# Order of the SwiGLU operands, banks of the last short products, and order of o's split behind two mixers

## The chip, the cores and the metric

The kernel runs on one core of a Trainium2 chip. The metric is the time of one execution on the device in microseconds (us); the median of several executions is compared. The core has a matmul engine (TensorE, PE in the profile, with its weight loads as PEld), a vector engine (VectorE, DVE), an engine for activations and copies (ScalarE, ACT), GpSimd (POOL), and SyncE (SP), on whose queue nearly all DMAs are issued. Each engine works its own instructions in the order in which they are queued.

## The reference

Two groups of tokens (512 and 256, together T = 768) go through a trunk of two layers with shared weights and model width 1024, all in 32-bit floats:

```python
def even_layer(x, ...):                       # layer 0
    x = x + 0.5 * swiglu(rmsnorm(x, f1_n), f1_g, f1_u, f1_d)
    x = x + mixer_ab(rmsnorm(x, mix_n), w_in, ..., w_out)
    x = x + 0.5 * swiglu(rmsnorm(x, f2_n), f2_g, f2_u, f2_d)
def odd_layer(x, ...):                        # layer 1
    x = x + 0.5 * swiglu(rmsnorm(x, f1_n), f1_g, f1_u, f1_d)
    x = x + mixer_c(rmsnorm(x, mix_n), w_qkv, rpb, w_out)
    x = x + 0.5 * swiglu(rmsnorm(x, f2_n), f2_g, f2_u, f2_d)
def swiglu(h, wg, wu, wd):
    return (silu(h @ wg) * (h @ wu)) @ wd     # hidden width 2816
```

A last RMS norm follows. `mixer_ab` is a spatial gating unit beside windowed attention, with one input and one output projection; `mixer_c` is neighbourhood attention on a grid. Each mixer ends with `o @ w_out` (1024 x 1024) and the addition to x.

## The kernel before

Activations lie transposed: x is eight tiles `x[m]` of 128 features by 768 tokens. The tokens fall into two halves of 384 (`HALVES`, h = 0 and 1). Every float operand of a matmul is split into a high part (a cast on ScalarE, L111, L193 or L340) and a low part (a subtraction on VectorE, L112, L194 or L341), and a product is three matmuls: high by high, low by high, high by low (`mm3`, L173). Weights come by DMA into four buffers (`raw`, L89) and are split into five buffers of high and low halves (`wsplit`, L101).

**SwiGLU** (`ffn`, L391) multiplies by a scheme of Strassen's kind with seven products of half size per pair of hidden tiles. Its operands are made from x: `b11` and `b21` from the first half of the tokens, and `t2`, `t3`, `t1`, `n4` and `b22` that need the second half. `feed` (L312) makes `b11` or `b21` for h = 0; for h = 1 it makes a tile `tmp` (a subtraction on VectorE, L327, for m below 4, a scaling on ScalarE, L329, for the others), and where both tiles of a k are there, it combines them (VectorE, L348) and splits the result into `t2`. `rest` (L350) makes `t3`, `t1`, `n4` and `b22` step by step. All `tmp` tiles, the copies named next and others share one set of `NE` = 30 buffers (`etile`, L309).

The opening of a SwiGLU is `ORDER`: for pairs 0 and 1 the product p1 (with `b11`, for gate and up, two products each), then p2 (with `b21`) for pairs 0 and 1, then the first hidden values of pair 0 (`hidden`, L475), p1 of pair 2, and so on. p1 leaves its result in a PSUM bank ("X"); ScalarE copies it to an `etile` for later use (L497), since p2 then adds onto the same bank. These copies are kept in a list, `self.copied`. After the opening pair 0 goes on with p6 (`t2`), p7 (`t3`), p5 (`t1`), p3 (`b22`), p4 (`n4`).

**What sets the order.** TensorE's instructions run in the order in which the program text issues them. Side work (norms, `rest`, attention) consists of generators that are resumed between matmuls, when a running estimate of TensorE's time (`self.t`) says so: each yields the time until its next step (`spawn`, `tick`). The instructions of the other engines are ordered at compile time by a planner, which takes what is ready, by priority, and priority falls in the order of issue; a block `high_priority` raises it (the copies of L497 and the weight halves for `b11` and `b21` have it). `issue_after(ins)` puts what is issued inside it behind `ins`, on the engine of `ins`.

**The end of a mixer** (`mixer_out`, L792). The mixer's result is `ot`, eight tiles o of 768 tokens. `ready(k)` (L802) splits o_k into `oh` and `ol`, first its first half and then its second, takes a new tile `x[k]` in the place of o_k and, behind the first mixer, issues the DMA that reloads x (L807). The first six k are made ready, and six tiles m of the output are computed from them for both halves (`put`, L809, adds x). When attention has ended, the last two k are made ready. Tiles m = 6 and 7 are computed whole. Then come the **short products**: for each half and each of the first six m, the share of the last two k (six matmuls), which VectorE adds to x (L861), and `final` (L696), which feeds the SwiGLU and sums squares (L216, L217). All take their bank from the pool `mm` (four banks); the other pool, `aux`, also has four. `half_done(h)` (L714) starts the norm of that half and, for h = 1, runs the eight feeds at once and spawns `rest`. In the mixers' case the second half's feeds can't run inside `final`, because the pool that they write is opened later; they are noted in `self.unfed`. The first SwiGLU of the program has a path of its own (`second`, L371), which waits until two copies are issued and puts its feeds and sums of squares behind the second.

Of the kernel before, what the change touches and what calls it, by code (L numbers as in the profile page):

```python
# [9 lines left out]
F32 = mybir.dt.float32  # L10
# [6 lines left out]
P = 128  # L17
# [5 lines left out]
T = TA + TB  # L23
# [26 lines left out]
class Trunk:  # L50
# [294 lines left out]
    def combine(self, out, x, sign, m, other):  # L345

        g, op = (self.gain(m), ALU.subtract) if sign > 0 else (self.gain(m, self.ngains), ALU.add)
        self.nc.vector.scalar_tensor_tensor(out=out, in0=x, scalar=g, in1=other, op0=ALU.mult, op1=op)  # L348

    def rest(self):  # L350

        (a0, a1), (c0, c1) = HALVES
        yield STEPS[0]
        for n in ("t3", "t1", "n4", "b22"):
            for k in range(4):
                if n == "t1":
                    self.gain_split(n, k, self.tmp[k], k)
                elif n == "t3":
                    t = self.etile("tmp")
                    self.combine(t, self.x[k][:, c0:c1], -1, k, self.tmp[k + 4])  # L360
                    self.split(*self.b[n][k], t)
                elif n == "n4":
                    t = self.tmp["t2", k]
                    self.combine(t, self.x[k + 4][:, a0:a1], 1, k + 4, t)
                    self.split(*self.b[n][k], t)
                else:
                    self.split(*self.b[n][k], self.tmp[k + 4])
                yield STEPS[1]
            self.made += [n]
# [344 lines left out]
    def half_done(self, h):  # L714

        if self.nxt[0] == "last":
            self.spawn(self.finish(h))
        else:
            self.spawn(self.norm_rt(h))
            if h:  # L720
                for m in self.unfed:
                    self.feed(m, h)
                self.spawn(self.rest())

    def finish(self, h):
# [66 lines left out]
    def mixer_out(self, name, ot, chain, cols=False):  # L792

        nc = self.nc
        oh, ol = ([self.gp.tile([P, T], F32R, tag=f"x{n}{k}", name=f"o{n}{k}") for k in range(KD)] for n in "hl")
        src = (oh, ol)
        self.x = [None] * KD
        old = {}  # L800

        def ready(k):  # L802
            for c0, c1 in HALVES:
                self.split(oh[k][:, c0:c1], ol[k][:, c0:c1], ot[k][:, c0:c1])
            self.x[k] = self.xp.tile([P, T], F32, tag=f"x{k}", name=f"x{k}")
            if not cols:
                nc.sync.dma_start(self.x[k], self.xd[k])  # L807

        def put(m, h, ps):  # L809

            c0, c1 = HALVES[h]
            x = self.x[m]
            parts = [(c0, c1, x[:, c0:c1], 0)]
            if cols:
                if m not in old:
                    t = self.rawp.tile([P, T], F32, tag="raw", name="xold")
                    nc.sync.dma_start(t, self.xd[m])
                    old.clear()
                    old[m] = [t[:, a:b].rearrange("p (r c) -> p c r", c=64) for a, b in GROUPS]
                a, b = old[m]  # L820
                parts = [(H, TA, a[:, 48:64, :], 8), (TA, T, b, 4)] if h else [(0, H, a[:, 0:48, :], 8)]
            for a, b, xv, rows in parts:
                out, pv = x[:, a:b], ps[:, a - c0 : b - c0]
                if rows:
                    out, pv = (t.rearrange("p (c r) -> p c r", r=rows) for t in (out, pv))
                nc.vector.tensor_tensor(out=out, in0=pv, in1=xv, op=ALU.add)

        early = range(KD - 2)
        for k in early:
            ready(k)  # L830
        for m in early:
            if m % 2 == 0:
                w4 = self.raw(name, 0, 4, m * P, 2 * P)
                w2 = self.unit(name, 4, 2, m * P, 2 * P)
            c = m % 2 * P
            hi, lo = self.wsplit(w4[:, :, c : c + P])
            w = [(hi[:, k, :], lo[:, k, :]) for k in range(4)] + [tuple(t[:, c : c + P] for t in k) for k in w2]
            for h in (0, 1):
                put(m, h, self.proj(w, src, HALVES[h], ks=early))
        self.drain(chain)  # L840
        late = (KD - 2, KD - 1)
        for k in late:
            ready(k)
        self.ffn_open(self.close("mp"))
        self.ffn_tiles()
        self.norm_begin(self.following)
        for m in late:
            wl = self.unit(name, 0, KD, m * P, P)
            for h in (0, 1) if m < KD - 1 else (0,):
                put(m, h, self.proj(wl, src, HALVES[h]))  # L850
                self.final(m, *HALVES[h])
        w = []
        for m, n in ((0, 4), (4, 2)):
            raw = self.raw(name, KD - 2, 2, m * P, n * P)
            w += [self.wsplit(raw[:, :, c : c + 2 * P]) for c in range(0, n * P, 2 * P)]
        for h, (c0, c1) in enumerate(HALVES):
            for m in early:
                st = [tuple(t[:, k, m % 2 * P : m % 2 * P + P] for t in w[m // 2]) for k in (0, 1)]
                ps = self.proj([None] * 6 + st, src, (c0, c1), ks=late)
                x = self.x[m][:, c0:c1]  # L860
                nc.vector.tensor_tensor(out=x, in0=ps[:, :H], in1=x, op=ALU.add)  # L861
                self.final(m, c0, c1)
            if h:
                put(KD - 1, h, self.proj(wl, src, (c0, c1)))
                self.final(KD - 1, c0, c1)
                self.close("xg")
                self.fw = self.open("work", self.other(self.guards["comb"][1]))
            self.half_done(h)
# [691 lines left out]
```

## Time and profile before

| | us |
|---|---|
| median of 3 runs | 2659.05 |
| lowest and highest run | 2657.87 and 2660.11 |
| the profiled execution | 2661.16 |
| its span, first to last instruction | 2659.4 |
| TensorE busy in the span | 2582.3 |
| VectorE busy | 2262.8 |
| ScalarE busy | 1371.3 |

The profile is that of one execution. Times are from the start of the span. A row of a timeline gives start, duration, engine, line, operation, the tile written and the tiles read, and in brackets how long the engine sat idle before it and what ended that. Duration overlaps with the next instruction, so the pitch from start to start is shorter: matmuls of 384 columns that last 0.34 us follow each other every 0.17. Names of tiles are those of the program without their running numbers: `b110h` is the high part of `b11`, k = 0. The granted clock is the share of full speed at which TensorE was let run; over the whole span it was 0.987. The first mixer ends near 785 us, the second near 2141 us; the first SwiGLU opens the span.

### The profile page before, as it was taken

What the parts mean: (1) busy time and instruction counts of PE and PEld (TensorE: products, weight loads), DVE (VectorE), ACT (ScalarE), POOL (GpSimd) and SP (SyncE); (2) the same over time, 40 slices, a digit from 0 to 9 for tenths busy, and PEclk for the clock granted to TensorE, in tenths of its full rate; (3) what the DMA queues carried; (4) which work ended last, traced back from release to release, by engine and by line L of the source; (5) the groups of instructions that cost most, each with busy time, mean ns of one, the idle gap of its engine ahead of it and who ended that gap; (6) DMA issues with size and microseconds to landing.
All of it is one profiled execution on the core that took longest, in us unless ns stands there. A gap on an engine that the chain in (4) does not pass through costs nothing.

```text
span 2659.4 us, 41163 instructions
## 1 busy us (share of the span) xinstructions
PE 2582.3 (97%) x15150; PEld 2513.1 (94%) x15150; DVE 2262.8 (85%) x4748; ACT 1371.3 (52%) x2847; POOL 82.7 (3%) x124
## 2 busy tenths in 40 slices
PE   7999999999999999999999999999999989999997
PEld 6999999977889999999999999988998989999997
DVE  8989889779869988898998888886667699888886
ACT  6545444555746544445654544454555465454443
POOL 0000000000100000000000000002112100000000
PEclk9999999999999999999999999999999999999999
DMA  5333222421222222222222222232221322222221
GB/s 163 118 81 106 71 72 64 156 74 37 84 80 80 80 78 65 80 72 88 80 80 80 64 80 64 82 123 64 62 62 44 100 88 80 80 71 73 67 86 55
DMA packets 82746, 214.80 MB, mean 81 GB/s; under 512 B 19952, under 2 KB 32752, under 8 KB 82544
## 3 DMA queue, kind: packets, MB, share of 16 engines
q1 hardware_dynamic: 82400, 212.14, 26.0%
q8 instruction: 119, 1.95, 0.3%
q14 instruction: 83, 0.68, 0.1%
q10 hardware_dynamic: 144, 0.03, 0.0%
HBM read 202.70 MB, written 15.07 MB: 82 GB/s over the span
## 4 chain that ended last, share of the span: by engine, by line
PE 91%; DVE 5%; ACT 3%; DMA 0%; issue 0%; SPq 0%; DVEq 0%; ACTq 0%
PE ps_mm L137 59%; PE ps_aux L137 32%; PE ps_aux L141 1%; DVE wlo L112 1%; DVE xl L710 1%; ACT whi L111 0%; DMA raw<-in_w 0%; ACT xh L709 0%; DVE x L677 0%; DVE ol L194 0%; ACT sq L216 0%; DVE x L632 0%; ACT p L883 0%; ACT diag L247 0%; DVE tmp L348 0%
## 5 line engine op out<-in xcount | busy, mean ns | idle before, releaser
L111 ACT CAST whi<-s 128x512 fp32r<-128x512 f32 x496 | 302.0, 620 | 378.5 <-DVE s L580 141.2
L111 ACT CAST whi<-raw 128x512 fp32r<-128x512 f32 x512 | 311.7, 618 | 272.4 <-PE ps_mm L137 135.9
L112 DVE TENSOR_TENSOR wlo<-s,whi 128x512 fp32r<-128x512 f32 x496 | 335.1, 685 | 73.2 <-ACT whi L111 72.9
L112 DVE TENSOR_TENSOR wlo<-raw,whi 128x512 fp32r<-128x512 f32 x494 | 336.7, 687 | 33.9 <-ACT whi L111 30.9
L137 PE MATMUL ps_aux<-dt,whi 128*128 128x384 f32 x864 | 221.5, 338 | 0.0
L137 PE MATMUL ps_mm<-db,whi 128*128 128x384 f32 x864 | 221.5, 338 | 0.0
L137 PEld LDWEIGHTS ps_mm<-db,whi 128*128 128x128 f32 x864 | 156.8, 188 | 0.0
L137 PEld LDWEIGHTS ps_aux<-dt,whi 128*128 128x128 f32 x864 | 156.8, 188 | 0.0
L137 PE MATMUL ps_mm<-xh,whi 128*128 128x512 f32 (+1 forms) x416 | 146.8, 353 | 3.0 <-ACT xh L709 3.0
L137 PE MATMUL ps_mm<-db,wlo 128*128 128x384 f32 x432 | 146.0, 338 | 0.0
L137 PE MATMUL ps_aux<-dt,wlo 128*128 128x384 f32 x432 | 146.0, 338 | 0.0
L137 PE MATMUL ps_mm<-xl,whi 128*128 128x512 f32 (+1 forms) x416 | 142.7, 343 | 1.1 <-DVE xl L710 1.1
L137 PE MATMUL ps_mm<-xh,wlo 128*128 128x512 f32 (+1 forms) x416 | 142.3, 342 | 0.0
L467 ACT COPY u<-ps_mm 128x384 f32<-128x384 f32 x176 | 83.6, 475 | 34.5 <-PE ps_mm L137 34.2
L472 DVE TENSOR_TENSOR u<-ps_aux,u 128x384 f32<-128x384 f32 x176 | 96.9, 551 | 5.0 <-PE ps_aux L137 3.9
L580 DVE TENSOR_TENSOR s<-raw,raw 128x512 f32<-128x512 f32 x124 | 83.3, 685 | 20.9 <-DMA raw<-in_w 20.9
L580 DVE TENSOR_TENSOR s<-raw 128x512 f32<-128x512 f32 x124 | 84.8, 685 | 17.2 <-DMA raw<-in_w 16.9
L137 PE MATMUL ps_aux<-dh,whi 128*128 128x384 f32 x384 | 98.5, 338 | 0.7 <-DVE x L677 0.7
L883 ACT ACTIVATE p<-p,st 128x256 f32<-128x256 f32 (+3 forms) x144 | 69.1, 481 | 53.3 <-DVE st L878 53.2
L632 DVE TENSOR_TENSOR x<-ps_aux,x 128x384 f32<-128x384 f32 x160 | 86.3, 552 | 10.9 <-PE ps_aux L137 10.8
L137 PE MATMUL ps_mm<-oh,whi 128*128 128x384 f32 x256 | 90.2, 352 | 5.1 <-DVE x L861 4.0
L137 PEld LDWEIGHTS ps_mm<-xh,whi 128*128 128x128 f32 x416 | 79.4, 191 | 14.2 <-ACT xh L709 4.1
(427 smaller groups left out, 8098.2 us busy)
## 6 DMA issues: line engine op xcount, KB each, us to landing
raw<-in_w SPq DMA_DIRECT2D x342, 512.0 KB, 3.7
xdm<-x SPq DMA_DIRECT2D x16, 384.0 KB, 2.3
x<-in_x SPq DMA_DIRECT2D x16, 192.0 KB, 5.7
x<-xdm SPq DMA_DIRECT2D x8, 384.0 KB, 3.6
xold<-xdm SPq DMA_DIRECT2D x8, 384.0 KB, 3.1
out_y<-y SPq DMA_DIRECT2D x8, 384.0 KB, 2.5
tab<-skew SPq DMA_DIRECT2D x8, 256.0 KB, 4.6
raw<-in_w SPq DMA_DIRECT2D x8, 256.0 KB, 2.6
```

Source lines behind the costliest of these rows:

```text
L111: nc.scalar.copy(hi, src)
L112: (eng or nc.gpsimd).tensor_tensor(out=lo, in0=src, in1=hi.bitcast(F32), op=ALU.subtract)
L137: self.nc.tensor.matmul(out, lhsT=lhsT, rhs=rhs, start=start, stop=stop, **kw)
L141: self.nc.tensor.transpose(out, src, self.ident)
L467: nc.scalar.copy(e[n, out], bank[key, n])
L472: nc.vector.tensor_tensor(out=t, in0=bank[key, n], in1=t, op=ALU.add)
L580: f = lambda o, x, y, op: self.nc.vector.tensor_tensor(out=o, in0=x, in1=y, op=op)
L632: nc.vector.tensor_tensor(out=o, in0=ps, in1=o, op=ALU.add)
L710: nc.vector.scalar_tensor_tensor(out=lo, in0=src, scalar=gain, in1=hi.bitcast(F32), op0=ALU.mult, op1=ALU.subtract)
L883: nc.scalar.activation(outs[i - n0], outs[i - n0], AF.Exp, scale=-1.0, bias=mn[:, i : i + 1], accum_out=sm[:, i : i + 1])
```

## The change

Three edits, all behind or at the end of the mixers:

1. `half_done` no longer runs the noted feeds at once. It spawns `late_feeds`, which waits until two more copies of L497 have been issued, issues the eight feeds behind the second of them (on ScalarE by an explicit order, on the other engines by the order of issue), and then goes on with `rest`. Where nothing was noted, `rest` is spawned as before.
2. `ready` takes a list of k. It splits the first half of every o in the list, then the second halves, and only then takes the x tiles and issues the reloads.
3. The short products of odd m take their bank from `aux`, those of even m from `mm`.

```diff
+    def late_feeds(self, n):
+
+        while len(self.copied) < n:
+            yield 0.2
+        with self.tc.issue_after(self.copied[n - 1]):
+            for m in self.unfed:
+                self.feed(m, 1)
+        yield from self.rest()
+
     def rest(self):
...
             self.spawn(self.norm_rt(h))
-            if h:
-                for m in self.unfed:
-                    self.feed(m, h)
+            if h and self.unfed:
+                self.spawn(self.late_feeds(len(self.copied) + 2))
+            elif h:
                 self.spawn(self.rest())
...
-        def ready(k):
+        def ready(ks):
             for c0, c1 in HALVES:
-                self.split(oh[k][:, c0:c1], ol[k][:, c0:c1], ot[k][:, c0:c1])
-            self.x[k] = self.xp.tile([P, T], F32, tag=f"x{k}", name=f"x{k}")
-            if not cols:
-                nc.sync.dma_start(self.x[k], self.xd[k])
+                for k in ks:
+                    self.split(oh[k][:, c0:c1], ol[k][:, c0:c1], ot[k][:, c0:c1])
+            for k in ks:
+                self.x[k] = self.xp.tile([P, T], F32, tag=f"x{k}", name=f"x{k}")
+                if not cols:
+                    nc.sync.dma_start(self.x[k], self.xd[k])
...
         early = range(KD - 2)
-        for k in early:
-            ready(k)
+        ready(early)
...
         late = (KD - 2, KD - 1)
-        for k in late:
-            ready(k)
+        ready(late)
...
-                ps = self.proj([None] * 6 + st, src, (c0, c1), ks=late)
+                ps = self.proj([None] * 6 + st, src, (c0, c1), self.psum(self.aux, "aux") if m % 2 else None, late)
```

## The prediction

> **What bounds the kernel now.** I read the page first, then TensorE's waits around the ends of the two mixers, then the windows there, and last the timelines of single engines. On the page TensorE is the bound, and the chain that ended last is nearly all matmuls:
>
> ```profile
> PE 2582.3 (97%) x15150; PEld 2513.1 (94%) x15150; DVE 2262.8 (85%) x4748; ACT 1371.3 (52%) x2847; POOL 82.7 (3%) x124
> ...
> PE 91%; DVE 5%; ACT 3%; DMA 0%; issue 0%; SPq 0%; DVEq 0%; ACTq 0%
> ```
>
> The matmuls stay the same, so only TensorE's 77 us without work (2659.4 - 2582.3) and its time at a slow clock can be won. What TensorE waits for behind the first mixer (690 to 860 us; columns: total us, times, longest):
>
> ```profile
> PE ps_mm L137 <- ACT p L497: 4.2, 1, 4.2
> PE ps_mm L137 <- DVE x L861: 2.0, 2, 1.8
> PE ps_mm L137 <- DVE ol L194: 1.1, 3, 0.6
> PE ps_mm L137 <- ACT oh L193: 1.1, 1, 1.1
> ```
>
> Behind the second (2040 to 2200 us):
>
> ```profile
> PE ps_mm L137 <- ACT p L497: 4.7, 1, 4.7
> PE ps_mm L137 <- DVE x L861: 2.0, 2, 1.8
> ...
> PE ps_mm L137 <- DVE ol L194: 0.5, 1, 0.5
> ```
>
> The three edits aim at these: the copies of the first products (L497), the adds that free the banks of the short products (L861), the split of o (L193, L194). The windows of both places (stretch, length, then PE, PEld, DVE, ACT and POOL busy, granted clock, DMA) show what a wait costs beside itself, and what VectorE does meanwhile:
>
> ```profile
> 764.00:785.30 21.30, 19.29 (x103) 18.65 (x102) 18.50 (x41) 11.98 (x24) 0.00 (x0) 0.92 0.04 17
> 785.30:808.30 23.00, 18.85 (x100) 18.53 (x99) 22.77 (x56) 19.74 (x41) 0.00 (x0) 0.93 0.31 102
> 808.30:824.30 16.00, 15.98 (x93) 15.37 (x92) 13.90 (x30) 8.83 (x19) 0.00 (x0) 1.00 0.17 52
> 2120.00:2140.90 20.90, 18.89 (x101) 18.25 (x100) 18.42 (x41) 12.38 (x25) 0.00 (x0) 0.92 0.07 28
> 2140.90:2166.20 25.30, 20.60 (x102) 20.23 (x101) 24.33 (x58) 20.02 (x41) 0.00 (x0) 0.87 0.38 125
> 2166.20:2182.00 15.80, 15.80 (x95) 15.80 (x95) 15.42 (x35) 9.33 (x19) 0.00 (x0) 1.00 0.21 63
> ```
>
> TensorE pauses 2.01 (21.30 - 19.29) and 4.15 us behind the first mixer, 2.01 and 4.70 behind the second, and around each pause its clock is down: 19.29 x 0.08 = 1.5, 18.85 x 0.07 = 1.3, 18.89 x 0.08 = 1.5, 20.60 x 0.13 = 2.7 us lost. That is 9.0 and 10.9 us of TensorE's time. But VectorE is idle for only 2.80 + 0.23 + 2.10 = 5.13 us in the first three stretches and 2.48 + 0.97 + 0.38 = 3.83 in the others. It is the engine that comes next.
>
> **The change, part by part.** No instruction is added or removed; the order and the banks change.
>
> *The feeds.* The four first products run from 785.33 to about 793.65, so one takes 2.08 us; the first copy starts only at 797.44. ScalarE, 19.74 of 23.00 us busy there, has it in line behind feeds. Behind the first mixer, and in the opening SwiGLU, such a late copy comes just after VectorE's fourth combine of the feeds (L348):
>
> ```profile
> 785.33 0.34 PE L137 MATMUL ps_mm<-b110h,whi 128*128 128x384 f32 x1
> 793.48 0.34 PE L137 MATMUL ps_mm<-b113h,wlo 128*128 128x384 f32 x1
> 797.33 0.60 DVE L348 SCALAR_TENSOR_TENSOR tmp<-tmp,ngains 128x384 f32<-128x384 f32 x1
> 797.44 0.48 ACT L497 COPY p<-ps_mm 128x384 f32<-128x384 f32 x1
> ...
> 15.28 0.48 ACT L497 COPY p<-ps_mm 128x384 f32<-128x384 f32 x1
> 29.70 0.61 DVE L348 SCALAR_TENSOR_TENSOR tmp<-tmp,ngains 128x384 f32<-128x384 f32 x1
> 29.82 0.46 ACT L497 COPY p<-ps_mm 128x384 f32<-128x384 f32 x1
> 30.34 0.69 PE L137 MATMUL ps_mm<-b210h,whi 128*128 128x384 f32 x1 [6.01 <-ACT p L497]
> ```
>
> Copies and feeds write the same set of 30 buffers, and I infer that a copy does not get its buffer before the feeds issued ahead of it. The change issues two copies first and the twelve feed buffers after them, as the opening does: there the second copy is prompt (15.28), and the third waits for the feeds. So the first copy's 4.15 and 4.70 us go, and the **third copy** is late next. Queued on ScalarE behind the second copy are four scalings and four casts of the feeds, then the sixteen of `rest`; TensorE asks for these only after twelve products. The third copy is due after six products, 12.5 us from the first one's start, 13.1 with the norm's two matmuls. The second copy ends at 4.2 + 0.5; then the feeds need VectorE for 4 x 0.47 + 4 x 0.53 us (the pitch of instructions that take 0.55 and 0.61), 1.4 for three low parts in between and 1.8 to 2.4 for weight halves: 7.2 to 7.8, so the third copy starts at 11.9 to 12.5. I take no wait for it; the other bound is the opening's, 29.82 - 15.28 = 14.5 us behind the second copy, so at 18.7 and over 5 us of wait.
>
> *The banks.* Twelve short products of 1.04 us (six matmuls) meet four banks, while in the first half VectorE needs about 1.5 us for each (an add, a low part, a sum of 0.47 to 0.53 us pitch):
>
> ```profile
> 765.11 0.56 DVE L861 TENSOR_TENSOR x<-ps_mm,x 128x384 f32<-128x384 f32 x1 [0.48 <-PE ps_mm L137]
> 776.72 0.45 PE L137 MATMUL ps_mm<-oh,whi 128*128 128x384 f32 x1 [1.80 <-DVE x L861]
> 778.31 0.52 PE L137 MATMUL ps_mm<-ol,whi 128*128 128x384 f32 x1
> ...
> 2120.61 0.56 DVE L861 TENSOR_TENSOR x<-ps_mm,x 128x384 f32<-128x384 f32 x1 [0.20 <-PE ps_mm L137]
> ```
>
> With eight banks TensorE runs ahead: 2.01 + 1.5 = 3.5 us sooner at the first product, behind either mixer. The second pool was the attention's, which has ended by then, so using it costs nothing; were it not free, a bank wait of up to 1.8 us would stay.
>
> After this pause of 1.80 us the matmuls take 0.52 us, not 0.34. The Trainium skill (TensorE: Matmul & The Clock Gate, Part 1: The HAM clock gate) puts the fall to half rate behind an idle window of about 3.4 us. By that rule this pause costs only itself, and taking it away would win 2.0 us per mixer in place of 3.5; the row has slow matmuls after 1.80 us, so the measurement decides.
>
> *The split of o.* TensorE's first product wants the first halves of six o's; now each o's second half stands in between. Removed: up to 1.1 + 1.1 us at the first mixer and 0.5 at the second; nothing, if the second halves are then late instead. I take 1.8 + 0.2, near the upper end, because the first six slots of both engines then hold what the first product wants. The reloads of x are issued behind all splits, and the next weights stand behind them in SP's queue:
>
> ```profile
> 699.95 9.76 SPq L807 DMA_DIRECT2D x<-xdm  x6
> ```
>
> The sixth reload waits for the same last split as now, so the queue clears at the same time. The first goes some 4 us later; four free banks hide that, and without them the first add would be late by about as much.
>
> *Where the gain of the first two stops.* VectorE's feed work can start only behind the second copy, and TensorE takes weight halves hot from VectorE:
>
> ```profile
> 787.23 0.55 DVE L327 TENSOR_TENSOR tmp<-x 128x384 f32<-128x384 f32 x1
> 813.46 0.69 DVE L580 TENSOR_TENSOR s<-raw 128x512 f32<-128x512 f32 x1 [2.10 <-DMA raw<-in_w]
> 823.59 0.68 DVE L112 TENSOR_TENSOR wlo<-s,whi 128x512 fp32r<-128x512 f32 x1
> 824.32 0.44 PE L137 MATMUL ps_mm<-t30h,wlo 128*128 128x384 f32 x1
> ...
> 2179.15 0.68 DVE L112 TENSOR_TENSOR wlo<-s,whi 128x512 fp32r<-128x512 f32 x1
> 2181.27 0.34 PE L137 MATMUL ps_mm<-t30h,wlo 128*128 128x384 f32 x1
> ```
>
> The half written until 824.27 is used at 824.32: no slack, with nearly all feed work ahead of it on VectorE, and, by the order of issue, still ahead of it after the change. So at this point TensorE can win only what VectorE loses of idle time, not 9.0 us. Of the 5.13 I leave 0.48 ahead of the first add and half of the 2.10 for a weight DMA, whose buffer comes free with TensorE's progress: 3.6. Of the second's 3.83 I leave 0.20 and half of 0.97 + 0.38: 2.95; there the same half is ready 1.4 us before its use, of which I add half: 3.7. Both could be 0, or the full 9.0 and 10.9.
>
> Sum: 2.0 + 3.6 + 3.7 = 9.3 us. The profiled execution took 2661.16 us (its span of 2659.4 and 1.8 around it), so 2651.9 of its kind. It lies 2.1 above the median of the runs shown, 2659.05; from the median, **2649.8**.
>
> **Rivals.** *All waits vanish.* If the work of `rest` falls behind the urgent halves, VectorE is no bound: 9.0 + 10.9 + 2.7 (all of the split) = 22.6 us, 2636.5. For it: `rest` is issued more than two products later than now. Against: the hot half at 824.27.
>
> *VectorE is held as well*, so that the change moves the waits and little else. The products start at 785.33 - 3.5 = 781.8, the second copy ends at 786.5, a scaling of 0.5 us leads the feeds: they start on VectorE at 787.0, against 787.23 now. If nothing fills VectorE until then, its idle time only moves, and 2.0 + 0.2 + 0.7 stay: 2656.2. For it: the feed buffers are taken in order, and a scaling on ScalarE has the first. Against: the norm's short chain and two weight halves are ready to fill the hole.
>
> *The opening's course*, the slower side. There the third copy holds TensorE for 6.01 us, and what follows is late as well:
>
> ```profile
> 19.32 0.72 PE L137 MATMUL ps_aux<-ones,acc 128*128 128x1 f32 x6
> 33.22 0.55 DVE L217 TENSOR_TENSOR acc<-acc,sq 128x384 f32<-128x384 f32 x1
> 59.81 0.34 PE L137 MATMUL ps_aux<-t10h,whi 128*128 128x384 f32 x1
> ...
> 826.16 0.34 PE L137 MATMUL ps_aux<-t10h,whi 128*128 128x384 f32 x1
> ...
> 2183.00 0.34 PE L137 MATMUL ps_aux<-t10h,whi 128*128 128x384 f32 x1
> ```
>
> From the end of the four first products to t1's product the opening takes 59.81 - 19.32 = 40.5 us, the mixers 826.16 - 793.65 = 32.5 and 2183.00 - 2149.3 = 33.7. At the opening's pace the change would lose 8.0 + 6.8 = 14.8 us there and win 7.0 (banks) and 2.0 (split): 5.8 slower, 2664.9. It decides from where the third copy starts more than some 10 us behind the second. Against: the opening still sums squares then (L217, until 33.22), which the mixers' ends have done before.
>
> **Chances and range.** Forecast (5.3 to 14 us won) 0.50; all waits vanish 0.17; VectorE held 0.25; the opening's course 0.08. About 0.2%, 5.3 us, is what a measurement of this kernel can tell from no change. Faster 0.67 is the first two, same 0.26 the third and a little of the last, slower 0.07. The range, 2641 to 2658, holds the forecast's own (2645 to 2653.7), the held case, and the lower part of the first rival.
>
> **What would show it.** Right: no wait on L861; first and second copies within 1 us of their products; VectorE over 97% busy from the first product to t3's, and TensorE waiting in that stretch for hidden values, weight halves or the third copy; no wait on oh over 0.5 us. Wrong: no such waits at all (then near 2637), or a wait of 5 us or more for the third copy on either side (then no gain, or slower).

## The result and the profile after

| kernel | median, us | range, us | ratio to before, 95% interval |
|---|---|---|---|
| before | 2658.42 | 2655.55 to 2660.11 | |
| after | 2650.89 | 2649.77 to 2652.01 | 0.9970 (0.9961 to 0.9978) |

The change is 7.5 us faster; the forecast was 2649.8. The two profiled spans differ by 9.2 us (2659.4 to 2650.2). The page of the kernel after, its busy times and its chain:

```profile
PE 2574.1 (97%) x15150; PEld 2503.7 (94%) x15150; DVE 2259.8 (85%) x4748; ACT 1371.4 (52%) x2847; POOL 82.9 (3%) x124
...
PE 89%; DVE 7%; ACT 2%; issue 1%; DMA 1%; SPq 0%; DVEq 0%; ACTq 0%
```

TensorE is busy 8.2 us less for the same matmuls, and its time without work is 76.1 us (2650.2 - 2574.1) where it was 77.1: in this pair of traces most of the gain is clock, and the waits have changed places more than they have gone. The granted clock over the whole span, pauses included, points the same way in every execution: 0.990 to 0.991 in the eight of the kernel after, 0.986 to 0.990 in the 103 of the kernel before that were timed beside the experiments. In the chain VectorE has more (7% in place of 5%). What TensorE waits for behind the first mixer (680 to 860 us):

```profile
PE ps_mm L137 <- ACT p L506: 2.6, 1, 2.6
PE ps_mm L137 <- ACT oh L193: 1.4, 1, 1.4
PE ps_mm L137 <- DVE wlo L112: 1.3, 2, 1.0
PE ps_mm L137 <- DVE sg L490: 0.8, 1, 0.8
```

and behind the second (2030 to 2200 us):

```profile
PE ps_mm L137 <- ACT whi L111: 1.9, 1, 1.9
...
PE ps_mm L137 <- DVE sg L490: 1.4, 1, 1.4
PE ps_mm L137 <- DVE wlo L112: 1.4, 2, 1.0
...
PE ps_mm L137 <- ACT p L506: 0.4, 1, 0.4
```

The waits on banks (the adds, now L870) and for the first copies (now L506) are gone. In their place stand the third copy, hidden values (sg), weight halves (wlo), and behind the second mixer weights (whi). Their places, with the copies in front of them, in the timeline of the kernel after:

```profile
779.43 0.34 PE L137 MATMUL ps_mm<-b110h,whi 128*128 128x384 f32 x1
782.19 0.48 ACT L506 COPY p<-ps_mm 128x384 f32<-128x384 f32 x1
784.15 0.47 ACT L506 COPY p<-ps_mm 128x384 f32<-128x384 f32 x1
786.04 0.55 DVE L217 TENSOR_TENSOR acc<-acc,sq 128x384 f32<-128x384 f32 x1
790.47 0.60 DVE L341 SCALAR_TENSOR_TENSOR t10l<-tmp,gains,t10h 128x384 fp32r<-128x384 f32 x1
794.82 0.61 DVE L348 SCALAR_TENSOR_TENSOR tmp<-tmp,ngains 128x384 f32<-128x384 f32 x1
795.25 0.47 ACT L506 COPY p<-ps_mm 128x384 f32<-128x384 f32 x1
795.77 0.44 PE L137 MATMUL ps_mm<-b210h,whi 128*128 128x384 f32 x1 [2.65 <-ACT p L506]
801.04 0.44 PE L137 MATMUL ps_mm<-b110h,whi 128*128 128x384 f32 x1 [0.83 <-DVE sg L490]
818.97 0.45 PE L137 MATMUL ps_mm<-t30h,wlo 128*128 128x384 f32 x1
...
2130.00 0.34 PE L137 MATMUL ps_mm<-b110h,whi 128*128 128x384 f32 x1
2138.38 0.44 PE L137 MATMUL ps_mm<-b110h,whi 128*128 128x384 f32 x1 [1.86 <-ACT whi L111]
2171.47 0.44 PE L137 MATMUL ps_mm<-t30h,wlo 128*128 128x384 f32 x1
```

Set beside the same matmuls before (785.33, 824.32, 2140.9 and 2181.27 in the prediction), TensorE reaches the first product 5.9 us sooner, and t3's second product, where the hot half is used, 5.35 us sooner; at the second mixer 10.9 and 9.8, of which 6.7 were there when its short products began. Each mixer wins and then gives a part back.

To see what VectorE did in that, take the stretch from the first short products to t3's second product, cut at the same matmuls in both kernels. Before:

```profile
763.17:824.32 61.15, 54.95 (x297) 53.37 (x296) 55.19 (x125) 40.57 (x83) 0.00 (x0) 0.94 0.18 60
2113.83:2181.26 67.43, 60.72 (x325) 59.71 (x325) 58.77 (x133) 42.54 (x87) 2.59 (x2) 0.92 0.26 82
```

After, with the stretch from the first product to t3 (for the second mixer to just behind it) once more by itself, in two parts:

```profile
761.42:818.97 57.55, 52.25 (x297) 50.20 (x296) 54.92 (x129) 41.04 (x84) 0.00 (x0) 1.00 0.22 64
2107.12:2171.47 64.35, 59.11 (x325) 56.73 (x324) 56.49 (x132) 41.94 (x86) 2.58 (x2) 0.97 0.25 82
...
779.40:801.00 21.60, 17.76 (x100) 16.80 (x98) 21.34 (x54) 18.60 (x40) 0.00 (x0) 1.00 0.47 126
801.00:816.50 15.50, 14.16 (x80) 13.38 (x80) 14.95 (x34) 10.11 (x20) 0.00 (x0) 1.00 0.08 30
2129.40:2152.90 23.50, 20.36 (x103) 19.06 (x101) 21.64 (x53) 18.41 (x40) 0.00 (x0) 0.93 0.42 140
2152.90:2170.30 17.40, 15.38 (x87) 14.61 (x88) 16.87 (x40) 11.17 (x22) 0.00 (x0) 1.00 0.06 24
```

The first stretch is 3.60 us shorter (TensorE waits 0.9 us less in it, and 2.7 are clock), and VectorE's idle time in it fell from 5.96 to 2.63 us: nearly all of the gain. The second is 3.08 us shorter, but VectorE's idle time fell only from 8.66 to 7.86. There 2.28 us of VectorE's work are no longer in the stretch. With 1.3 us from the split the two make 8.0 us. The rest of the 9.2 lies outside: 0.4 us ahead of the first mixer's end, 1.4 between the two stretches, and 0.6 lost behind the second; one trace of each kernel can't tell what of that comes from the edits.

Cut once more at the first product, TensorE gains 4.15 us at either mixer from the first short product to there, and loses 0.55 and 1.1 us from there to t3's product, where it waits longer than before (5.3 us in place of 4.2, and 5.2 in place of 4.7). All that the two stretches gain arises ahead of the first products; putting the feeds later keeps more of it than the banks alone keep (below).

### The profile page after: what moved, and what is told of

The parts are those of the page before. It is cut to its first block, busy times and chain, and to the rows that moved or that the text cites. A ratio compares the mean times of both kernels' runs of the same rounds, so it can differ in the third digit from the quotient of the medians.

```text
span 2650.2 us, 41138 instructions
## 1 busy us (share of the span) xinstructions
PE 2574.1 (97%) x15150; PEld 2503.7 (94%) x15150; DVE 2259.8 (85%) x4748; ACT 1371.4 (52%) x2847; POOL 82.9 (3%) x124
## 4 chain that ended last, share of the span: by engine, by line
PE 89%; DVE 7%; ACT 2%; issue 1%; DMA 1%; SPq 0%; DVEq 0%; ACTq 0%
PE ps_mm L137 56%; PE ps_aux L137 32%; DVE wlo L112 1%; PE ps_aux L141 1%; DVE x L641 1%; DVE s L589 1%; DVE xl L719 1%; DMA raw<-in_w 1%; DVE tmp L348 0%; ACT whi L111 0%; ACT xh L718 0%; DVE x L686 0%; ACT sq L216 0%; ACT p L892 0%; DVE sg L493 0%
## 5 line engine op out<-in xcount | busy, mean ns | idle before, releaser
L641 DVE TENSOR_TENSOR x<-ps_mm,x 128x384 f32<-128x384 f32 x160 | 87.1, 551 | 6.0 <-PE ps_mm L137 5.8
```

Source lines behind the costliest of these rows:

```text
L641: nc.vector.tensor_tensor(out=o, in0=ps, in1=o, op=ALU.add)
```

## The experiments

Each was timed beside the kernel before on the same chip (its median there 2659.3 to 2659.5, for the last run 2657.8). Two theories stand against each other in most of them: that VectorE's load sets the end of these stretches (A), and that single waits do, each of which can be taken away (the rivals).

**The split alone.** Only the diff's `ready` is applied.

> The kernel before with only the split of o changed (all first halves, then all second halves, then the reloads of x). Theory A, that the term stands by itself: the shift of TensorE's matmuls between the two profiles was 1.3 us in front of the first mixer's first product (and 0.2 at the second), so 2656.9 to 2657.0 beside 2658.4. The prediction's own term was 2.0, so 2656.4. Rival: the first mixer's gain is eaten by what comes next (a bank's add late by the later reload of x, or the feeds), no difference within 0.5 us; then waits on L861 grow by about what the waits on oh and ol lost.

Measured: 2656.85, ratio 0.9990 (0.9981 to 0.9999). By the same matmuls of both traces the step at the first mixer's products is 1.35 us, at the second 0: there the wait for ol (0.5 us) went, but one for the attention's row values (st, L878) grew from 0.7 to 1.6 us, as it did in the kernel after. The waits on L861 did not grow (2.0 us at either mixer), so the rival's sign is missing. The rest of the measured difference cannot be told from its interval.

**The banks alone.**

```diff
-                ps = self.proj([None] * 6 + st, src, (c0, c1), ks=late)
+                ps = self.proj([None] * 6 + st, src, (c0, c1), self.psum(self.aux, "aux") if m % 2 else None, late)
```

> The kernel before with only the second PSUM pool for every other short product. Theory A (VectorE is the next bound and the first copy stays behind the feeds): TensorE comes 3.5 to 4.2 us sooner to the first product behind each mixer, but the wait for the first copy (4.2 and 4.7 us) grows by what VectorE cannot gain; VectorE has 2.80 and 2.48 us of idle time there, so 1.5 to 2.3 us per mixer stay: 3 to 4.6 us in all, 2653.8 to 2655.4. Rival B (the banks' gain is TensorE's own and stays): 4.2 + 4.2 = 8.4, near 2650. Rival C (the copy's wait grows by all of it): no difference within 1 us, first copy at the same time as before.

Measured: 2657.60, ratio 0.9994 (0.9985 to 1.0002). Its waits, first mixer and then second:

```profile
PE ps_mm L137 <- ACT p L497: 6.7, 1, 6.7
...
PE ps_mm L137 <- ACT p L497: 5.3, 1, 5.3
PE ps_mm L137 <- ACT whi L111: 1.4, 1, 1.4
```

The first copy's wait grew from 4.2 to 6.7 and from 4.7 to 5.3 us, and the wait for weights appears behind the second mixer. About 2 us per mixer are left of the 4.15 by the same matmuls, as theory A has it; B, 8.4 us, falls. The time alone does not tell A from C, but in the trace the first copy behind the first mixer starts 1.6 us sooner, counted from the first short product, where C has it at the same time.

**The feeds alone.** `late_feeds` and its call are applied; banks and split are as before.

> The kernel before with only the feeds put behind the second copy. Theory A (VectorE is the next bound): the first copy's waits (4.15 and 4.70 us) go, but TensorE waits again behind them (third copy, hidden values, weight halves) and keeps only VectorE's idle time there, 0.23 + 1.05 and 1.15, so 1.3 to 2.5 us in all: 2656 to 2657. Rival B (waits and slow clock of these stretches are all won): 4.15 + 1.3 + 4.70 + 2.7 = 12.9, 2645.5. Rival C: without the banks VectorE has to wait for the second copy with nothing to do (its feeds now start behind it), so that the time is as before or up to 2 us longer.

Measured: 2658.27, ratio 0.9997 (0.9988 to 1.0006). B falls. Its waits, first mixer and then second:

```profile
PE ps_mm L137 <- DVE sg L490: 1.7, 1, 1.7
...
PE ps_mm L137 <- ACT p L506: 4.4, 1, 4.4
```

By the same matmuls the first mixer's stretch is 2.8 us shorter. But 1.6 of these lie ahead of the first product, where the edit changes nothing: there a pause on a bank was followed by the slow clock in the trace before and not in this one (last section). That leaves 1.2 us for the feeds. Behind the second mixer the third copy now holds TensorE for 4.4 us, nearly what the first copy did before (4.7), and that stretch became 1.8 us longer (69.23 against 67.43). This is the rival of the opening's course in small. The time does not tell A from C. With the banks, in the kernel after, the third copy's wait there is 0.4.

The three ratios together are 0.0019 below one, the change 0.0030; with 0.0009 of uncertainty on each, it can't be told whether the parts add.

**Own buffers for the copies.** Four buffers that the down projection uses only later take the first four copies, in the kernel before and in the kernel after:

```diff
-                        e[n, "p1"] = etile("p1")
+                        j = 2 * p + names.index(n)
+                        e[n, "p1"] = etile("p1") if j > 3 else self.fw.tile([P, H], F32, tag=f"p1{j}", name=f"p1{j}")
```

> The kernel before, with the feeds where they were, but the copies of the first four first products written to four buffers that the down projection uses only later, not to the 30 shared with the feeds. Theory of the shared buffers: the copies are then prompt (each within 1.5 us of its product's end) though the feeds are issued ahead of them, in the opening too, where the third copy holds TensorE for 6.0 us. Rival: the copies stand behind the feeds for another reason (ScalarE's line); then the first copy behind the mixer still starts just after the fourth combine and the time does not move. If the copies are prompt: with VectorE as the next bound 2 to 6 us less than before (2652 to 2656); if TensorE alone counts 4.15 + 4.70 + 6.0 and the clock, 15 us or more (2643 or less).

Measured: 2657.08, ratio 0.9995 (0.9986 to 1.0004). Its timeline, the opening and then behind the first mixer:

```profile
17.84 0.47 ACT L498 COPY p<-ps_mm 128x384 f32<-128x384 f32 x1
34.29 0.69 PE L137 MATMUL ps_aux<-diag,onesr 128*128 128x384 f32 x1 [5.72 <-DVE diag L249]
...
788.22 0.48 ACT L498 COPY p<-ps_mm 128x384 f32<-128x384 f32 x1
805.20 0.44 PE L137 MATMUL ps_mm<-b110h,whi 128*128 128x384 f32 x1 [1.21 <-DVE sg L481]
```

The copies are prompt although the feeds are still issued ahead of them: 788.22 in place of 797.44 behind the mixer, and in the opening the third one at 17.84 in place of 29.82. So the shared buffers did set the order. In the opening the 6.01 us for the third copy became 5.72 for the norm's matrix: nothing is won there. The 15 us that were to come if TensorE's waits alone count did not, and the interval (at most 3.7 us won) leaves only the lower end of the 2 to 6 us.

> The kernel after, with the copies of the first four first products in four buffers of their own (those of the down projection's sums). If shared buffers put the third copy behind the feeds, it is now within 1.5 us of its product's end and its wait of 2.65 us behind the first mixer (0.4 behind the second) and of 6.0 us in the opening goes. Theory A (VectorE next): the waits for hidden values and weight halves grow by nearly as much, 0.997 again, at most 1 us less. Rival D (the third copy's place is what costs): 2.6 + 0.4 us or more less, 0.9955 to 0.996. In the opening both expect nothing, as the wait for the norm took all of it back.

Measured: 2653.68, ratio 0.9981 (0.9972 to 0.9990). The waits for the third copy are gone, and this one stands in their place behind the first mixer:

```profile
801.20 0.49 PE L137 MATMUL ps_mm<-b110h,whi 128*128 128x384 f32 x1 [3.33 <-DVE sg L490]
```

2.65 + 0.83 us before the third pair's first product became 3.33: D falls.

**Low parts on GpSimd**, which is idle there:

```diff
-                    self.split(*self.b[n][k], t)
+                    self.split(*self.b[n][k], t, eng)
```

(`eng` is `nc.gpsimd` behind the mixers only; n4, and b22 in the same way. `split` gives it the subtraction, not the cast.)

> The kernel after, with the low parts of n4 and b22 behind the two mixers computed on GpSimd in place of VectorE (8 x 0.47 = 3.8 us off VectorE per mixer; about 1.0 us each on GpSimd by the row of the last norm). The kernel after stands at 0.997 of before. Theory A (VectorE is the bound from the first products to t3): TensorE wins 2 to 4 us per mixer more, in the waits for hidden values and weight halves (0.8 + 1.3 us behind the first, 1.4 + 1.4 behind the second, and clock), ratio 0.995 to 0.996. Rival D (ScalarE's line is the bound, since the third copy waits behind 19 scalings and casts with no idle time on ScalarE): the third copy's 2.65 us stay and the time does not move, 0.997. Rival E: GpSimd slows VectorE or is itself late for b22, waits on b22 or n4 over 1 us, 0.998 or more.

Measured: 2658.58, ratio 0.9997 (0.9988 to 1.0006): the change's gain is gone. VectorE and GpSimd in that run, and the first stretch (761.82 to 822.70 by the same matmuls):

```profile
796.57 1.35 POOL L194 TENSOR_TENSOR b220l<-tmp,b220h 128x384 fp32r<-128x384 f32 x1 [8.68 <-ACT b220h L193]
796.97 1.37 DVE L348 SCALAR_TENSOR_TENSOR tmp<-x,ngains,tmp 128x384 f32<-128x384 f32 x1
...
798.26 1.36 DVE L194 TENSOR_TENSOR t23l<-tmp,t23h 128x384 fp32r<-128x384 f32 x1
809.12 0.55 DVE L490 TENSOR_TENSOR sg<-ps_mm,acc 128x384 f32<-128x384 f32 x1
...
761.82:822.70 60.88, 54.06 (x298) 51.89 (x297) 58.80 (x122) 41.63 (x85) 10.57 (x8) 0.97 0.23 68
```

The VectorE instructions of 384 columns with both inputs in SBUF that start while GpSimd works take about 1.36 us in place of 0.55 to 0.61. The one at 809.12, which takes an input from PSUM, started while GpSimd worked (808.10 to 810.09) and took 0.55. VectorE lost more than it was spared: it is busy 58.80 us, 3.9 more than in the kernel after, and the stretch is 3.3 longer. This is rival E, and at the same time a load added to VectorE that TensorE had to wait out.

**Later work.** On ScalarE t1's scalings are put behind the fourth copy, and the casts of n4 and b22 behind the sixth (`first` is the third copy's place in the list):

```diff
+            if first and n != "t3":
+                i = first + (1 if n == "t1" else 3)
+                while len(self.copied) <= i:
+                    yield 0.2
+                behind = lambda i=i: self.tc.issue_after(self.copied[i])
             for k in range(4):
+              with behind():
```

> The kernel after, with the scalings and casts of t1 behind the fourth copy and those of n4 and b22 behind the sixth on ScalarE. No work is saved; 5.9 us of VectorE work per mixer (n4's four combines, eight low parts) and ten casts leave the stretch up to t3. Theory A (VectorE bound in that stretch, but not behind it): TensorE wins 2 to 5 us per mixer, ratio 0.993 to 0.996, waits for the third copy, hidden values and weight halves mostly gone. Rival F (VectorE is as full behind t3): the waits come back at n4, b22 or the weight halves there, 0.997. Rival G: n4 or b22 late, waits over 2 us on them, 0.998 or more.

Measured: 2652.37, ratio 0.9973 (0.9964 to 0.9982), as the kernel after. VectorE and TensorE there:

```profile
794.50 2.49 DVE L112 TENSOR_TENSOR wlo<-raw,whi 128x512 fp32r<-128x512 f32 x4
799.90 0.55 DVE L194 TENSOR_TENSOR t33l<-tmp,t33h 128x384 fp32r<-128x384 f32 x1
800.37 0.55 DVE L497 TENSOR_TENSOR sg<-ps_mm,acc 128x384 f32<-128x384 f32 x1
801.06 0.47 PE L137 MATMUL ps_mm<-b110h,whi 128*128 128x384 f32 x1 [4.01 <-DVE sg L497]
```

Behind the first mixer the third copy and the weight halves hold nothing up now; sg does, 4.0 us, behind t3's work in VectorE's order. The 2 to 5 us per mixer of theory A did not come.

> Both: n4 and b22 late and their low parts on GpSimd. Theory A: as the better of the two, or up to 2 us more, 0.992 to 0.995. Rival F (load behind t3 limits the late order): this one is clearly (over 2 us) below the late order alone. Rival D (ScalarE's line): equal to the late order alone within 1 us.

Measured: 2660.82, ratio 1.0005 (0.9996 to 1.0014). GpSimd costs as much as in the run above, 8.5 us over the late order alone. None of the three theories had that sign.

**t3 behind sg.** VectorE does t3's combines and low parts only after the first pair's sg and v (`self.hid` lists the instructions that write v).

```diff
+        while len(self.hid) <= i:
+            yield 0.2
+        yield from self.rest(self.hid[i])
...
+              with self.tc.issue_after(behind) if behind and n == "t3" else nullcontext():
```

> The kernel after, with t3's combines and low parts put behind the first pair's hidden multiplies (sg and v) in VectorE's order, behind both mixers. No work is saved or taken out of the stretch up to t3. Theory A (VectorE's load up to t3 sets the end): the waits for sg (0.8 and 1.4 us) go and come back at the weight halves or at t3, ratio 0.9965 to 0.9975 as the kernel after. Theory H (it is VectorE's order: sg stands in line behind values that are needed more than 10 us later): 2 to 4 us less than the kernel after, 0.9955 to 0.9963, no wait on sg and none on t3 over 0.5 us.

Measured: 2658.83, ratio 0.9999 (0.9990 to 1.0008). Its waits behind the first mixer up to 900 us, its first stretch, and what follows:

```profile
PE ps_mm L138 <- ACT whi L112: 4.5, 4, 1.5
...
761.11:816.71 55.60, 51.72 (x297) 50.44 (x297) 53.06 (x122) 40.03 (x82) 0.00 (x0) 1.00 0.23 66
816.71:838.03 21.32, 18.54 (x99) 16.64 (x98) 20.52 (x49) 9.89 (x22) 0.00 (x0) 1.00 0.38 109
```

sg's wait went, and TensorE was 2 us quicker up to t3 (55.60 against 57.55). Behind it VectorE is still full (20.52 of 21.32), sums of weights are late, and TensorE waits for their casts: both theories fall, the work only changes its place, at a loss.

> The late order of t1, n4 and b22, and t3 behind sg and v. In the late order alone TensorE waited 4.0 and 3.3 us for sg and the third copy no more, and the weight halves before t3 hardly (0 and 0.4 us). Theory A (load up to t3): with n4 and b22 gone from that stretch VectorE has room, so 7.3 us of waits and about 2 us of slow clock are won: 4 to 8 us less than the kernel after, 0.994 to 0.9955. Theory H says the same. Rival F (VectorE as full behind t3, where n4 and b22 now stand): waits on t1, n4, b22 or weight halves behind t3 come to 5 us or more and the ratio stays at 0.997.

Measured: 2661.43, ratio 1.0002 (0.9993 to 1.0010).

> The same, with the first four copies in buffers of their own. The late order has taken the third copy's wait already, so within 1 us of the run without own buffers behind the mixers; in the opening the 6.0 us wait moves to the norm's matrix (as in the two runs with own buffers, where nothing stayed). If the shared buffers still cost something behind the mixers, 1 us or more less.

Measured: 2660.94, ratio 1.0007 (0.9999 to 1.0016). In both the same waits for whi appear (5.4 and 5.1 us from 680 to 900 us). Of the first, rival F holds, and worse than it said; the second lies within 1 us of the first, as expected, so the shared buffers cost nothing measurable there.

**Less work for VectorE.** Twelve low parts per mixer are left out:

```diff
+                if less and n != "t3":
...
+                    self.b[n][k] = (hi, self.b["b11"][k][1])
```

> The kernel after, where behind both mixers the low parts of t1, n4 and b22 are left out (the products take the low part of b11 instead, which lies there already): twelve VectorE instructions fewer per mixer, 4 x 0.53 + 8 x 0.47 = 5.9 us, and nothing else. In the compiled order sums of weights move up into the room, so sg stays about where it is. Theory A (VectorE's load from the first products to behind t3 sets the end): the waits for weight halves go (1.3 and 1.4 us) and what stands behind them comes sooner, 3 to 8 us less than the kernel after, ratio 0.994 to 0.996. Rival (single waits in a chain, not the load: third copy, sg, weights from memory): within 1.5 us of the kernel after, 0.9965 to 0.9975.

Measured: 2649.54, ratio 0.9967 (0.9955 to 0.9980): not told apart from the kernel after. Its first and second stretch, and its timeline:

```profile
760.76:819.06 58.30, 53.01 (x298) 52.06 (x297) 52.96 (x121) 41.55 (x85) 0.00 (x0) 0.97 0.21 66
2105.87:2168.29 62.42, 58.27 (x326) 56.89 (x325) 54.07 (x122) 42.44 (x87) 2.58 (x2) 0.97 0.28 93
...
791.88 0.69 DVE L600 TENSOR_TENSOR s<-raw 128x512 f32<-128x512 f32 x1 [2.01 <-DMA raw<-in_w]
796.69 0.66 PE L137 MATMUL ps_mm<-b210h,whi 128*128 128x384 f32 x1 [4.25 <-ACT p L517]
```

Behind the second mixer VectorE has 2.4 us less to do in the stretch, and the stretch is 1.9 us shorter. Behind the first, the compiled order put a sum of weights ahead of the feeds, and VectorE stood 2.01 us waiting for its transfer; the third copy's wait rose to 4.25 us and took the gain back. So the run speaks for the load at one place, is spoiled at the other, and the 3 to 8 us of theory A are not shown.

No version is measurably faster than the kernel after.

## Why the prediction was right, and where not

**The sum.** 9.3 us were predicted; the profiles differ by 9.2 and the medians by 7.5. The steps that can be placed in the traces make 8.0, so that 9.3 meets 9.2 is in part luck. The rivals "all waits vanish" (22.6), "VectorE is held" (2.9) and the opening's course (a loss) did not come about as wholes.

**The split.** Predicted 1.8 + 0.2, measured 1.3 + 0. The term was taken near its upper end, and the statement "no wait on oh over 0.5 us" was wrong: a wait of 1.4 us for a first half stands where 1.1 + 1.1 were. At the second mixer a wait of the attention took the place of the one that went.

**The banks.** No wait on the adds is left, so the second pool was free. Predicted 3.5 us at the first product; by the same matmuls it was 4.15 (5.90 less the 1.75 already won at 763.17) behind the first mixer and 4.2 behind the second. They are the 2.01 us of pauses, 1.6 of slow clock, and 0.55 more, which the sum did not have. From the first short product to the first product it took 22.15 us before and 18.01 after, but 20.57 in the three other traces with the old banks (split alone, feeds alone, own buffers in the kernel before), where no slow clock followed the pauses: 22.15 - 20.57 = 1.58, and 20.57 - 18.01 - 2.01 = 0.55. So the clock's 1.5 us were read rightly from this trace, but they are not there in every execution: with the old banks the pause of 1.8 us was followed by the slow clock at four of eight places. Where it is not, the banks win 2.6 us per mixer, less than the 3.5; the agreement in size is in part luck.

**The feeds.** Both first copies start within a microsecond of their products, and the shared buffers as the reason for the late ones are confirmed by the run with own buffers. The third copy was named as late next, but at no wait: it was to start 11.9 to 12.5 us behind the first product's start. It started at 15.8 (795.25 - 779.43), in between the two bounds, and cost 2.65 us at the first mixer and 0.4 at the second. There it was late as well, 14.1 us behind the first product's start (2144.10), but TensorE had been held up by whi before, so the 0.4 is no sign that the count was right. The count of VectorE's work ahead of the fourth combine (7.2 to 7.8 us) was the step that failed. From the second copy's end, 784.6, to that combine, 794.8, it was 10.2 us, because two sums of squares (L217, 0.9 us), two low parts of t1 (L341, 1.1 us), which the planner drew ahead, and the norm's small instructions (about 1.0 us), which the count left out, stand between the feeds.

**Where the gain stops.** For the first mixer 3.6 us were to stay, as much as VectorE could lose of its idle time. The stretch lost 3.60 and the idle time 3.33. The size was right and the working nearly so: VectorE lost 1.8 us of idle time ahead of the first product (2.3 were reckoned) and 1.5 behind it (1.3). That it came to 3.60 is in part luck: with the split alone this stretch took 60.39 us in place of 61.15, because the slow clock behind the 1.80 us pause did not come in that execution. From the first product to t3 VectorE is 98% busy, 36.3 of 37.1 us. For the second mixer 3.7 were predicted and 3.08 came, but the working was wrong: the idle time fell by 0.8 only, the other 2.28 us are work that is no longer ahead of t3's product. VectorE was 94% busy from the first product to t3 (38.51 of 40.90), not over 97%, and one wait was foreseen by no step, the 1.86 us for whi. The banks alone show it too (1.4 us), the split and the feeds alone do not, so it comes with an earlier first product.

**VectorE as the next bound** was too simple as a rule. For it speak the banks alone, the first stretch, and the run in which GpSimd slowed VectorE and TensorE waited it out. But to free VectorE or to reorder it won nothing: copies on ScalarE, sg, weight halves, sums and transfers lie within one to four microseconds of each other there, and each run that took one away met the next. What a kernel with less VectorE work and an order chosen for it would win was not run, and stays open.

## What to carry to other kernels

When TensorE stops waiting, look up what the next engine loses of its own idle time in the same stretch, cut at the same instructions: that, and not the waits removed, sized the gain at the first mixer here; at the second most of it was work that no longer stood ahead of the end. Look also at a second execution before a price is put on a slow clock. A wait that goes because work was put later comes back where that work is due, so count all of the work ahead of it in the engine's compiled order, not only that of the edited lines. Three edits that win 1 to 3 us each can hardly be told from no change one by one here; judge them together.

## What the runs showed of the hardware

**GpSimd and VectorE hold each other up.** Rows above: 1.36 us for a VectorE instruction that takes 0.55 to 0.61 alone, and 1.01 to 1.99 us for the eight on GpSimd there, where one of this size took 1.0 in the last norm of the kernel before. The Trainium skill (SBUF — State Buffer, Who interferes with whom) says that a VectorE instruction with two inputs in SBUF contends with a GpSimd instruction that reads SBUF, and calls their shared ports an exclusive lock. The trace agrees: the two slow rows end 0.4 us after the GpSimd instruction that they met (796.97 + 1.37 against 796.57 + 1.35), and the row with an input from PSUM was not slowed. The rule speaks against handing VectorE's work of that kind to GpSimd, and the expectations gave it too little weight.

**A short pause costs clock only at times.** Before, the pause of 1.80 us in front of 776.72 was followed by matmuls of 0.52 us (778.31). In the run with the feeds alone the same pause at the same place was not:

```profile
776.02 0.44 PE L137 MATMUL ps_mm<-oh,whi 128*128 128x384 f32 x1 [1.80 <-DVE x L870]
...
778.38 0.34 PE L137 MATMUL ps_mm<-ol,whi 128*128 128x384 f32 x1
```

With the old banks this pause, 1.77 to 1.80 us long, stands at eight places of four traces (before, split alone, feeds alone, own buffers in the kernel before): ten or eleven of the matmuls behind it follow each other every 0.320 us in place of 0.173 at four of them, none at the other four. Nor did the 2.65 us in front of 795.77 in the kernel after slow what followed (its window has clock 1.00), while the same wait with low parts on GpSimd, in front of 796.92, was followed by slow matmuls. So of the clock that one profile shows behind a pause, a part is that execution's chance; this may be why the profiles differ by more than the medians, which no run here settles.
